# Output projection of a hybrid decoder layer: sums of rows and a factor of the last products on VectorE in place of GpSimd

## The chip, the cores and the metric

The kernel runs on one core of one Trainium2 chip. The metric is the device time of one execution in microseconds (us). The engines in question are TensorE (PE, with PEld for loading its weights), VectorE (DVE), ScalarE (ACT) and GpSimd (POOL). SyncE (SP) issues most of the DMAs. Each engine works through its own list of instructions in order.

## The reference

One layer of a decoder for 2048 prompt tokens and 8 x 4 sample tokens of width 1024. Four groups of heads (convolution, pooling, stick-breaking attention, attention to a memory) each give 512 columns. They are concatenated, multiplied by `w_out`, normalised, added to the input, and normalised once more:

```python
h = rms_norm(x, pre_g); z = h @ w_in
...
mix = jnp.concatenate([y_c * jax.nn.silu(cg), y_p * jax.nn.silu(pg),
                       y_s * jax.nn.silu(sg), y_m * jax.nn.silu(mg)], axis=-1)   # rows x 2048
out = rms_norm(mix @ w_out, post_g)                                               # rows x 1024
x = x + out
...
y = rms_norm(x, final_g)
```

The change lies in `mix @ w_out` and in the factor `post_g` behind it. Nothing ahead of that is touched.

## The kernel before

The output projection is the last stage of the kernel. The 2048 prompt rows are 16 tiles of 128, taken as eight pairs, i = 0 to 7. (i = 8, `LAST`, stands for the 32 sample rows.) A pair of row tiles, the two halves of `mix`'s 2048 columns and the two halves of the 1024 result columns make a 2 x 2 block product, and the kernel computes it with seven block products in place of eight, in a form of Strassen's method: products 1, 7, 2, 6, 4, 5 and 3, whose inputs are blocks or sums of blocks. The sums of the blocks of `w_out` are made earlier. The rows of `mix` lie in DRAM (`mixd`). The row sums are made here, product by product:

- product 7 takes a difference of two blocks, made on POOL (line 1737) and stored to DRAM (`msd[0]`);
- product 6 takes a first difference of that stored one, made on DVE (line 1739, tile `mr6_i_h`);
- a second difference, of product 2's rows and the one of line 1739, is made on POOL (line 1740, tile `mr2_i_h`) and stored to DRAM (`msd[1]`), from where product 3 loads it later;
- product 5 takes the sum of two blocks which product 4's load has brought in one buffer. It is made on POOL (line 1733, tile `mr4_i_h`, the name of the buffer) inside `tc.issue_after(keep["sixth"])`, which keeps it in the order of the source behind the latest difference of line 1740.

In the names, the first number is the product, the second the pair i, the third h, which half of the K dimension (1024 columns, two times 512) it is.

Each input is split into two parts of reduced precision (fp32r), whose products add up to fp32. For the rows ACT rounds (line 1748, tile `mh`) and DVE subtracts (line 1759, tile `ml`); for the weights ACT rounds (line 1654, `wohi`) and DVE subtracts (line 1659, `wolo`). PE then runs three matmuls for each 128 columns of K (line 2024: hi x hi, lo weights x `mh`, hi weights x `ml`), so 12 for one (product, i, h) and 24 for one accumulator `acc`.

The order of the products is a list: product 1 for all i, then 7, then 2 and 6 in turn, then the last three, 4, 5 and 3, in turn pair by pair (from i = 3 on, 4, 5, 3 of a pair follow one another). Rows are loaded three parts ahead, sums made and rounded a few parts ahead. PE's list follows the order of the source. For the other engines a scheduling layer sorts what is recorded, by its estimate of when each instruction can run, unless `tc.keep_in_program_order` or `tc.issue_after` fixes it: the subtractions of line 1739 and the roundings and subtractions of the weights are fixed, while the subtractions of line 1759 are not.

Behind each accumulator DVE adds what the other products gave (lines 1794 to 1811, `U`, `c` and `acc`), ACT takes the sum of squares, and DVE multiplies by `gpost` (line 1816). Of the even row tiles, the first half of the result columns is done early (product 2), stored in DRAM (`c11d`) and loaded back as `oh2_i`; `out_factor` multiplies it by `gpost` on POOL (line 1844). Then `out_tile` finishes a row tile: root of the mean square (from tile 10 on, on POOL, lines 1857 and 1858), `x` + result (line 1868, twice, on DVE), a second root, and the final factor (line 1875, on DVE; `oxt` is the tile that goes out). POOL's other work in this time is these roots and sums of the convolution.

Of the kernel before, what the change touches and what calls it, by code (L numbers as in the profile page):

```python
# [13 lines left out]
ALU = mybir.AluOpType  # L14
# [78 lines left out]
def kernel(  # L93
# [9 lines left out]
    pe, act, dve, pool, sp = nc.tensor, nc.scalar, nc.vector, nc.gpsimd, nc.sync  # L103
# [1544 lines left out]
    def store(key=None):  # L1648
        while len(stores) > 2 or key in [k for k, *_ in stores]:
            sp.dma_start(*stores.pop(0)[1:])  # L1650
# [76 lines left out]
    def out_combine(x):  # L1727
        prod, i, h = x
        store()
        ts = raws[x]  # L1730
        if prod == 5 and i < LAST:
            with tc.issue_after(keep["sixth"]):
                pool.tensor_tensor(out=ts[1], in0=ts[0], in1=ts[1], op=ALU.add)
            ts = ts[1:]
        elif prod == 7:
            pool.tensor_tensor(out=ts[0], in0=ts[0], in1=ts[1], op=ALU.subtract)
            stores.append(((0, i, h), msd[0, i, h], ts[0]))
        elif prod == 6:
            tc.keep_in_program_order(dve.tensor_tensor(out=ts[0], in0=ts[0], in1=ts[1], op=ALU.subtract))
            keep["sixth"] = pool.tensor_tensor(out=ts[2], in0=ts[2], in1=ts[0], op=ALU.subtract).ins  # L1740
            stores.append(((1, i, h), msd[1, i, h], ts[2]))
        raws[x] = ts[0]

# [21 lines left out]
    def out_ready(prod, i, o):  # L1765
# [35 lines left out]
        else:  # L1801
# [28 lines left out]
            if prod == 5 and i != 2 or (prod, i) == (3, 1):  # L1830
                out_factor(2 if prod == 3 else i)
# [9 lines left out]
        keep[2 * i, 0] = c  # L1841

    def out_factor(i):
        pool.tensor_tensor(out=keep[2 * i, 0], in0=keep[2 * i, 0], in1=gpost[:, :512], op=ALU.mult)

    def out_tile(t, a, b):

# [130 lines left out]
    raws, mix, accs, keep, stores = {}, {}, {}, {}, []  # L1978
# [3 lines left out]
    def side_work():  # L1982
        nonlocal opm, conv
        with tc.tile_pool(name="sm", bufs=1, side="left", reuse_waits="tile") as sm2:
            yield from sample_end(sm2, side_ps, S)
        with tc.tile_pool(name="wsp", bufs=1, side="left", reuse_waits="tile") as wsp:
            yield from weight_sums(wsp)
        opm = ox.enter_context(tc.tile_pool(name="opm", bufs=1, side="left", reuse_waits="tile"))
        yield from out_weights(1, opm, pool)
        while (3, 0) not in flags:  # L1990
            yield
        for x in lead_:
            out_load(x)
            out_combine(x)
            out_high(x)
            out_low(x, pool)
            yield

        while (3, 1) not in flags:
            yield  # L2000
        for x in parts[2 * LEAD : 2 * LEAD + 3]:
            out_load(x)
        cp = cx.enter_context(tc.tile_pool(name="cp", bufs=1, side="left", reuse_waits="tile"))
        conv = conv_post(cp, lambda n: conv_ps[0](n), lambda: cx.enter_context(
            tc.tile_pool(name="cpw", bufs=1, side="left", reuse_waits="tile")))
        while "centered" not in flags:
            next(conv)
            yield
# [55 lines left out]
    op = oy.enter_context(tc.tile_pool(name="op", bufs=1, side="right", reuse_waits="tile"))  # L2064
# [58 lines left out]
    def prepare(n):  # L2123
        for d, f in ((3, out_load), (1, out_combine), (0, out_high)):
            for x in parts[: n + d]:
                if x in ready[d]:
                    continue
                prod, i, h = x
                if d == 3 and not h and prod == 2:
                    while i < LAST and ("conv", i) not in flags:  # L2130
                        next(conv, None)
                    if i == LAST:
                        for _ in conv:
                            pass
                f(x)
                ready[d].add(x)

    ready = {d: set(lead_ if d < 3 else parts[: 2 * LEAD + 3]) for d in (3, 1, 0, -1)}
    for n, x in enumerate(parts):
        if n == last_:  # L2140
# [3 lines left out]
            gpost = ope.tile([P, D], F32, name="gpost", bufs=1)  # L2144
# [4 lines left out]
        prod, i, h = x  # L2149
# [55 lines left out]
```

## Time and profile before

| | |
|---|---|
| median of 3 runs | 2327.63 us (2325.99, 2327.63, 2337.69) |
| the profiled execution's own time | 2329.11 us |
| its span | 2327.4 us |
| instructions in it | 43469 |
| HBM read, written | 465.35 MB, 90.72 MB |

The page's groups give for each kind of instruction: line, engine, operation, result <- inputs, how many, then busy time and mean length of one, and after the bar the idle time ahead of them with the engine or DMA that ended most of it. In a timeline a row begins with the start in us and the length; the brackets at its end hold the idle time ahead of the row and what released it. Two instructions merged in one row carry x2. The profile's busy share over 40 slices shows where in the span the stage lies: POOL, busy for most of the span, is at 20 to 40% in the last seven slices, from about 1920 us on:

```
PE   7999999999999999999999999999999999999997
DVE  5343786969647764477786867899999876686997
POOL 3554546556474655545546455489999964432332
```

### The profile page before, as it was taken

The numbers are of one execution on the slowest core, as the hardware profiler recorded it, in microseconds if no ns is written. First come the engines' busy times: TensorE is split into PE (matmuls) and PEld (weight loads), VectorE is DVE, ScalarE is ACT, GpSimd is POOL, SyncE is SP. The second block draws the span as 40 slices with busy tenths as digits, with TensorE's granted clock in tenths as the row PEclk, the third lists the DMA queues.
The fourth block names the chain that finished last, engine by engine and source line by source line (L and its number), as shares of the span: only waits on it lengthen the run. The fifth ranks groups of instructions, "written<-read, shape, count | busy, mean of one in ns | idle before, by whom it ended". The sixth has DMA issues, their size and how long they took to land. (4 is left out here: it accounts for less than half of the span.)

```text
span 2327.4 us, 43469 instructions
## 1 busy us (share of the span) xinstructions
PE 2252.0 (97%) x16512; PEld 1815.3 (78%) x16512; DVE 1716.6 (74%) x2303; ACT 1079.3 (46%) x1975; POOL 1317.9 (57%) x1410
## 2 busy tenths in 40 slices
PE   7999999999999999999999999999999999999997
PEld 7998888888888777777777777667766668787775
DVE  5343786969647764477786867899999876686997
ACT  5332343342442322224242334588888876453553
POOL 3554546556474655545546455489999964432332
PEclk9999999999999999999999999899999999999999
DMA  6689977878679899987977884666545207876774
GB/s 213 200 284 323 337 265 261 285 249 286 245 254 307 308 355 335 336 287 270 319 253 233 298 275 149 166 199 200 158 132 133 76 20 233 290 231 190 248 248 145
DMA packets 338189, 558.32 MB, mean 240 GB/s; under 512 B 29163, under 2 KB 213611, under 8 KB 321581
## 3 DMA queue, kind: packets, MB, share of 16 engines
q1 hardware_dynamic: 282604, 286.83, 39.8%
q0 software_dynamic: 55376, 268.72, 32.4%
q8 instruction: 130, 2.13, 0.4%
q14 instruction: 79, 0.64, 0.1%
HBM read 465.35 MB, written 90.72 MB: 239 GB/s over the span
## 5 line engine op out<-in xcount | busy, mean ns | idle before, releaser
L990 DVE STREAM_TRANSPOSE T<-kt 128x1024 f32<-128x1024 f32 x256 | 308.6, 1226 | 182.2 <-PE sSA L1003 174.7
L957 POOL DMA_INDIRECT vt<-in_cache_v_dram,idv x256 | 253.1, 989 | 257.0 <-PE sO L1042 195.9
L642 DVE SCALAR_TENSOR_TENSOR cacc<-U,par,cacc 128x512 f32<-128x512 f32 x480 | 359.8, 750 | 11.0
L1379 POOL TENSOR_TENSOR be<-be,E 128x512 f32<-128x512 f32 (+4 forms) x316 | 314.1, 1004 | 25.4 <-DVE E L1370 13.0
L957 POOL DMA_INDIRECT kt<-in_cache_k_dram,idk x128 | 128.7, 1006 | 196.1 <-DVE T L990 155.2
L1370 DVE TENSOR_TENSOR_SCAN E<-gam,cr,ZM 128x513 f32<-128x513 f32 x192 | 230.7, 1261 | 4.7 <-POOL csq L1490 1.0
L2024 PE MATMUL acc<-wohi,mh 128*128 128x512 f32 (+1 forms) x480 | 192.0, 400 | 0.2 <-ACT mh L1748 0.2
L2024 PE MATMUL acc<-wolo,mh 128*128 128x512 f32 (+1 forms) x480 | 188.4, 392 | 0.7 <-DVE wolo L1659 0.7
L2024 PE MATMUL acc<-wohi,ml 128*128 128x512 f32 x448 | 177.2, 395 | 6.5 <-DVE ml L1759 6.5
L1400 ACT COPY at<-AT 128x512 f32<-128x512 f32 (+1 forms) x288 | 154.6, 598 | 44.2 <-PE AT L1398 39.0
L1398 PE MATMUL AT<-ident,be 128*128 128x128 f32 x1082 | 155.9, 283 | 17.4 <-ACT at L1400 11.7
L1398 PEld LDWEIGHTS AT<-ident,be 128*128 128x128 f32 x1082 | 122.1, 144 | 59.6 <-issue 23.8
L1298 ACT ACTIVATE be<-S 128x1024 f32<-128x1024 f32 (+1 forms) x158 | 154.2, 976 | 9.9 <-PE S L1293 7.5
L1003 PE MATMUL sSA<-T,W 128*32 128x128 f32 x4096 | 138.2, 276 | 1.8 <-DVE T L990 1.4
L1410 PE MATMUL av<-at,V 128*64 128x256 f32 (+1 forms) x1152 | 137.0, 378 | 0.5 <-DVE sgt L1414 0.3
L1292 PE MATMUL S<-kh,Q 128*128 128x512 f32 (+1 forms) x316 | 134.6, 430 | 1.5 <-ACT be L1298 1.5
L1003 PEld LDWEIGHTS sSA<-T,W 128*32 128x32 f32 x4096 | 104.5, 109 | 36.7 <-issue 29.1
L1759 DVE TENSOR_TENSOR ml<-mr,mh 128x512 fp32r<-128x512 f32 x108 | 92.3, 862 | 40.4 <-ACT mh L1748 39.6
L1410 PEld LDWEIGHTS av<-at,V 128*64 128x64 f32 x1152 | 76.4, 138 | 58.4 <-issue 23.5
L1042 PE MATMUL sO<-vt,saT 128*32 128x512 f32 x1024 | 122.0, 592 | 0.0
L1293 PE MATMUL S<-kl,Q 66*128 66x512 f32 (+1 forms) x316 | 120.7, 386 | 0.0
L1748 ACT CAST mh<-mr 128x512 fp32r<-128x512 f32 (+1 forms) x120 | 70.3, 594 | 89.9 <-PE acc L2024 26.0
(591 smaller groups left out, 6254.5 us busy)
## 6 DMA issues: line engine op xcount, KB each, us to landing
mr<-mixd SPq DMA_DIRECT2D x32, 512.0 KB
Q<-qd SPq DMA_DIRECT2D x96, 128.0 KB
mr<-mixd SPq DMA_DIRECT2D x48, 256.0 KB
xtp<-in_x_prompt_dram SPq DMA_DIRECT2D x16, 512.0 KB
kh<-kd SPq DMA_DIRECT2D x64, 128.0 KB
ws<-in_w_out_dram SPq DMA_DIRECT2D x16, 512.0 KB
wsd<-ws SPq DMA_DIRECT2D x16, 512.0 KB
msd<-mr SPq DMA_DIRECT2D x32, 256.0 KB
```

Of the source, the lines that this page charges most:

```text
L642: dve.scalar_tensor_tensor(out=ps, in0=U[:, a + k : a + k + H], scalar=wd[:, k : k + 1], in1=ps, op0=ALU.mult, op1=ALU.add)
L957: pool.indirect_dma_start(out=dst, out_offset=None, in_=rows, in_offset=bass.IndirectOffsetOnAxis(ap=idx, axis=0))
L990: S["turn"] = dve.transpose(T[:, 2 * hh : 2 * hh + 2].rearrange("p s j t -> p (s j t)"), kt[:, 2 * hh : 2 * hh + 2].rearrange("p s j d -> ...
L1003: pe.matmul(sSs[n][32 * g : 32 * g + 32, P * ml : P * (ml + 1)], lhsT=W[:, jj, :], rhs=T[:, :, jj, :], start=i == 0, stop=i == 3, tile_pos ...
L1292: pe.matmul(S[:, j, :w], lhsT=Q[:, 0, c], rhs=kts[0][:, :w], start=True, stop=False)
L1298: act.activation(out=be, in_=S[:, :, :w], func=AF.Sigmoid)
L1370: dve.tensor_tensor_scan(out=E[:, j][:, ::-1], data0=g_[:, j][:, ::-1], data1=ZM[:, 0:1].to_broadcast([P, 513]), initial=carry[hh, q2][:, ...
L1379: newest.append(pool.tensor_tensor(out=be[:, j, :m], in0=be[:, j, :m], in1=E[:, j, 513 - w : 513 - w + m], op=ALU.mult).ins)
L1398: pe.transpose(ap_[:, n : n + P], A[hp, qb, kc, hh, qt][:, P * r : P * (r + 1)], ident)
L1400: act.copy(at[:, :n], ap_[:, :n])
L1410: pe.matmul(av[64 * hh : 64 * hh + 64, c], lhsT=V[:, 4 * kc + r, 64 * hh : 64 * hh + 64], rhs=ats.pop((hp, qb, kc, hh, q2, r)), start=dg a ...
L2024: pe.matmul(o[:rows], lhsT=m[a][:, k, :rows], rhs=W[prod, 4 * h + k][w], start=not cont and h == k == n == 0, stop=h == 1 and k == 3 and n ...
```

## The change

Three operations of the last products move from POOL to DVE, 40 instructions in all: the sum of product 5 (line 1733, 16 times), the second difference of product 6 (line 1740, 16 times) and the factor of the rows loaded back from DRAM (line 1844, 8 times). The sum of product 5 is also no longer kept behind the latest second difference; the scheduling layer is free to place all three. Nothing else is edited. One line goes, so line numbers behind it are one lower in the new kernel (1732, 1739 and 1843 for the three).

```diff
@@ -1729,15 +1729,14 @@
         store()
         ts = raws[x]
         if prod == 5 and i < LAST:
-            with tc.issue_after(keep["sixth"]):
-                pool.tensor_tensor(out=ts[1], in0=ts[0], in1=ts[1], op=ALU.add)
+            dve.tensor_tensor(out=ts[1], in0=ts[0], in1=ts[1], op=ALU.add)
             ts = ts[1:]
         elif prod == 7:
             pool.tensor_tensor(out=ts[0], in0=ts[0], in1=ts[1], op=ALU.subtract)
             stores.append(((0, i, h), msd[0, i, h], ts[0]))
         elif prod == 6:
             tc.keep_in_program_order(dve.tensor_tensor(out=ts[0], in0=ts[0], in1=ts[1], op=ALU.subtract))
-            keep["sixth"] = pool.tensor_tensor(out=ts[2], in0=ts[2], in1=ts[0], op=ALU.subtract).ins
+            dve.tensor_tensor(out=ts[2], in0=ts[2], in1=ts[0], op=ALU.subtract)
             stores.append(((1, i, h), msd[1, i, h], ts[2]))
         raws[x] = ts[0]
 
@@ -1841,7 +1840,7 @@
         keep[2 * i, 0] = c
 
     def out_factor(i):
-        pool.tensor_tensor(out=keep[2 * i, 0], in0=keep[2 * i, 0], in1=gpost[:, :512], op=ALU.mult)
+        dve.tensor_tensor(out=keep[2 * i, 0], in0=keep[2 * i, 0], in1=gpost[:, :512], op=ALU.mult)
 
     def out_tile(t, a, b):
```

PE's list is the same in both kernels, row by row. POOL's list has 40 rows fewer. DVE's has 40 more, and other rows around them are placed anew. The first difference in DVE's list stands at the first instruction of line 1739, at 2046 us of the profiled execution.

Place one is in DVE's list, ahead of the subtraction `ml6_7_1` for product 6 of the last pair. Before:

```order
L1739 TENSOR_TENSOR mr6_7_1_22850<-mr6_7_1_22850 128x512
L1659 TENSOR_TENSOR wolo4_6_22917<-wor4_6_22832,wohi4_6_22916 128x512
L1659 TENSOR_TENSOR wolo5_1_22922<-wor5_0_22834,wohi5_1_22921 128x512
L1759 TENSOR_TENSOR ml6_7_1_22940<-mr6_7_1_22850,mh6_7_1_22939 128x512
L1659 TENSOR_TENSOR wolo4_7_22946<-wor4_6_22832,wohi4_7_22945 128x512
L1659 TENSOR_TENSOR wolo5_2_22950<-wor5_2_22866,wohi5_2_22949 128x512
```

And in the new kernel (line 1732 is product 5's sum, line 1739 the second difference, line 1758 the subtraction for the rows):

```order
L1738 TENSOR_TENSOR mr6_7_1_22850<-mr6_7_1_22850 128x512
L1732 TENSOR_TENSOR mr4_0_0_22875<-mr4_0_0_22875 128x512
L1739 TENSOR_TENSOR mr2_7_1_22697<-mr2_7_1_22697,mr6_7_1_22850 128x512
L1659 TENSOR_TENSOR wolo4_6_22917<-wor4_6_22832,wohi4_6_22916 128x512
L1659 TENSOR_TENSOR wolo5_1_22922<-wor5_0_22834,wohi5_1_22921 128x512
L1659 TENSOR_TENSOR wolo4_7_22946<-wor4_6_22832,wohi4_7_22945 128x512
L1659 TENSOR_TENSOR wolo5_2_22950<-wor5_2_22866,wohi5_2_22949 128x512
L1758 TENSOR_TENSOR ml6_7_1_22940<-mr6_7_1_22850,mh6_7_1_22939 128x512
```

A row sum for product 4/5 and a second difference stand ahead of the subtraction now, and two subtractions of weights (`wolo4_7`, `wolo5_2`) that followed it precede it.

Place two is in DVE's list as well, from the end of tile 11 (`oxt11`) to the rows of pair 6. `acc3_5` is the accumulator of product 3 of pair 5; lines 1811 and 1816 add `U2` to it and multiply it by `gpost`. Before:

```order
L1868 SCALAR_TENSOR_TENSOR oxt11_23991<-acc4_5_23917,oss_23024,oxt11_23991 128x512
L1868 SCALAR_TENSOR_TENSOR oxt11_23991<-acc5_5_23956,oss_23024,oxt11_23991 128x512
L1759 TENSOR_TENSOR ml5_6_0_24059<-mr4_6_0_23931,mh5_6_0_24058 128x512
L1875 SCALAR_TENSOR_TENSOR oxt11_23991<-oxt11_23991,oss_23024,gfin_23021 128x1024
L1811 TENSOR_TENSOR acc3_5_24007<-acc3_5_24007,U2_20491 128x512
L1759 TENSOR_TENSOR ml5_6_1_24080<-mr4_6_1_23951,mh5_6_1_24079 128x512
L1816 TENSOR_TENSOR acc3_5_24007<-acc3_5_24007,gpost_23020 128x512
L1868 SCALAR_TENSOR_TENSOR oxt10_24043<-oh2_5_23915,oss_23024,oxt10_24043 128x512
L1868 SCALAR_TENSOR_TENSOR oxt10_24043<-acc3_5_24007,oss_23024,oxt10_24043 128x512
L1759 TENSOR_TENSOR ml3_6_0_24100<-mr3_6_0_24021,mh3_6_0_24099 128x512
```

In the new kernel (each line number one lower):

```order
L1867 SCALAR_TENSOR_TENSOR oxt11_23991<-acc4_5_23917,oss_23024,oxt11_23991 128x512
L1867 SCALAR_TENSOR_TENSOR oxt11_23991<-acc5_5_23956,oss_23024,oxt11_23991 128x512
L1810 TENSOR_TENSOR acc3_5_24007<-acc3_5_24007,U2_20491 128x512
L1732 TENSOR_TENSOR mr4_6_1_23951<-mr4_6_1_23951 128x512
L1874 SCALAR_TENSOR_TENSOR oxt11_23991<-oxt11_23991,oss_23024,gfin_23021 128x1024
L1815 TENSOR_TENSOR acc3_5_24007<-acc3_5_24007,gpost_23020 128x512
L1867 SCALAR_TENSOR_TENSOR oxt10_24043<-oh2_5_23915,oss_23024,oxt10_24043 128x512
L1867 SCALAR_TENSOR_TENSOR oxt10_24043<-acc3_5_24007,oss_23024,oxt10_24043 128x512
L1758 TENSOR_TENSOR ml5_6_0_24059<-mr4_6_0_23931,mh5_6_0_24058 128x512
L1758 TENSOR_TENSOR ml5_6_1_24080<-mr4_6_1_23951,mh5_6_1_24079 128x512
L1810 TENSOR_TENSOR acc4_6_24063<-acc4_6_24063,U3_20492 128x512
L1874 SCALAR_TENSOR_TENSOR oxt10_24043<-oxt10_24043,oss_23024,gfin_23021 128x1024
```

The sum for `mr4_6_1` is new on DVE here. The subtractions `ml5_6_0` and `ml5_6_1`, which stood apart among the operations on tiles 11 and 10, stand together behind the two instructions of line 1867 on tile 10, and the last factor of tile 11 (line 1874) comes ahead of both.

## Prediction

> **What bounds the kernel now.** I read the page first, then the busy time by stretches, PE's waits, the groups of VectorE (DVE) and GpSimd (POOL), and the timeline. Line numbers are those of before.
>
> ```profile
> PE 2252.0 (97%) x16512; PEld 1815.3 (78%) x16512; DVE 1716.6 (74%) x2303; ACT 1079.3 (46%) x1975; POOL 1317.9 (57%) x1410
> ```
>
> TensorE (PE) is busy nearly throughout. The order of every engine is unchanged up to DVE's first subtraction at L1739, at 2046 us, so only the last 281 us of the span can move. Columns below: stretch, its length, then busy time and instructions of PE, PEld, DVE, ACT, POOL, the granted clock, DMA share and GB/s.
>
> ```profile
> 2046.00:2100.00 54.00, 51.45 (x277) 43.70 (x276) 46.38 (x74) 28.69 (x59) 23.79 (x22) 1.00 0.73 226
> 2100.00:2161.00 61.00, 60.27 (x295) 49.16 (x295) 42.01 (x62) 22.89 (x47) 13.24 (x10) 1.00 0.72 221
> 2161.00:2200.00 39.00, 37.34 (x162) 29.81 (x160) 36.39 (x57) 22.87 (x48) 18.48 (x9) 1.00 0.72 241
> 2200.00:2250.00 50.00, 48.19 (x206) 36.93 (x207) 47.21 (x84) 27.97 (x78) 14.49 (x9) 1.00 0.71 241
> 2250.00:2314.00 64.00, 60.55 (x257) 47.32 (x255) 55.50 (x83) 28.54 (x76) 17.77 (x25) 1.00 0.54 192
> ```
>
> The clock is full. From 2161 on DVE is as busy as PE: 139.1 of 153 us. What PE itself waits for from 2046 to 2315 (us in total, times, longest):
>
> ```profile
> PE acc L2024 <- DVE ml L1759: 6.5, 10, 1.4
> PE cz L1535 <- DVE cgt L1538: 2.7, 2, 2.0
> PE acc L2024 <- DVE wolo L1659: 0.7, 1, 0.7
> PE acc L2024 <- ACT mh L1748: 0.2, 1, 0.2
> ```
>
> That is 10.1 us, nearly all on DVE. Its work otherwise is fixed, so **10.1 us is the most that this stage can give**. The end is PE's last run of products and the sums behind it:
>
> ```profile
> 2294.62 19.27 PE acc L2024 x82
> 2313.91 0.70 DVE og L1811
> ```
>
> 82 matmuls in 19.27 us are 0.235 each: what PE needs when nothing keeps it.
>
> **What is removed from POOL.** The three groups, with the idle time ahead of them:
>
> ```profile
> L1733 POOL TENSOR_TENSOR mr<-mr 128x512 f32<-128x512 f32 x16 | 27.1, 1707 | 55.0 <-DVE oxt L1868 28.3 <-DMA mr<-mixd 16.6 <-DVE acc L1816 8.8
> L1740 POOL TENSOR_TENSOR mr<-mr,mr 128x512 f32<-128x512 f32 x16 | 27.1, 1693 | 55.0 <-DVE mr L1739 47.7 <-ACT junk L1763 3.9 <-issue 2.7
> L1844 POOL TENSOR_TENSOR oh<-oh,gpost 128x512 f32<-128x512 f32 x8 | 12.4, 1554 | 19.4 <-DMA oh<-c11d 16.1 <-DVE oss L1860 1.7 <-DVE ml L1759 1.7
> ```
>
> Forty instructions, 66.6 us. POOL waits for others before them, and no row of PE's waits names POOL; their removal alone gives nothing there. What it gives is on DVE:
>
> ```profile
> 2167.79 5.24 POOL L1733 TENSOR_TENSOR mr<-mr 128x512 f32<-128x512 f32 x3
> 2168.30 1.77 DVE L1759 TENSOR_TENSOR ml<-mr,mh 128x512 fp32r<-128x512 f32 x1
> 2170.00 0.68 DVE L1794 TENSOR_TENSOR U<-acc,U 128x512 f32<-128x512 f32 x1
> ```
>
> While POOL works, a subtraction with both inputs in SBUF takes 1.77 us, and one that reads an accumulator stays at 0.68. DVE's groups from 2046 to 2314 say the same:
>
> ```profile
> L1759 DVE TENSOR_TENSOR ml<-mr,mh 128x512 fp32r<-128x512 f32 x77 | 65.8, 860 | 7.2 <-ACT mh L1748 6.7
> L1659 DVE TENSOR_TENSOR wolo<-wor,wohi 128x512 fp32r<-128x512 f32 x30 | 27.5, 940 | 1.2 <-ACT wohi L1654 1.1
> L1739 DVE TENSOR_TENSOR mr<-mr 128x512 f32<-128x512 f32 x16 | 13.1, 822 | 0.0
> L1875 DVE SCALAR_TENSOR_TENSOR oxt<-oxt,oss,gfin 128x1024 f32<-128x1024 f32 x14 | 21.1, 1507 | 4.3 <-POOL oss L1858 4.3
> L1739 DVE TENSOR_TENSOR mr<-mr x16: 673/680/1784, 2046.3 to 2160.0; 128x512 f32<-128x512 f32 x16
> ```
>
> The last row gives shortest, median and longest: 0.68 is the undisturbed length, and L1875 takes 1.28 undisturbed (row at 2291.60 below). The excess is 77 x 0.18 + 30 x 0.26 + 16 x 0.14 + 14 x 0.23 = 13.9 + 7.8 + 2.2 + 3.2 = 27.1 us. Of POOL's 87.8 us in this time 66.6 belong to the moved groups (76%), the rest to convolution sums and roots that stay. So the relief is between 20.6 and 27.1 us; I take 24, the middle, since smaller groups that I left out are stretched too.
>
> [...]
>
> **What is added to DVE.** Forty additions, subtractions and products of 128x512. In an undisturbed run of DVE one follows the other every 0.60 us, though each is shown with 0.68:
>
> ```profile
> 2178.34 0.68 DVE L1759 TENSOR_TENSOR ml<-mr,mh 128x512 fp32r<-128x512 f32 x1
> 2178.94 0.67 DVE L1784 TENSOR_TENSOR both<-both,gpost 32x512 f32<-32x512 f32 x1
> 2179.54 0.68 DVE L1811 TENSOR_TENSOR acc<-acc,U 128x512 f32<-128x512 f32 x1
> ```
>
> 40 x 0.60 = 24.0 us, 24 of them (14.4 us) after 2161. Against 24 us of relief **DVE's load stays as it is, within some 4 us**. Time can then only come from where the load lies: before, 1.1 us falls on whichever subtraction is at work; now 0.6 lies where the order puts it. I walked two places.
>
> Place one, the second subtraction for product 6 of pair 7. PE waits there and just behind; the three long DVE rows are the stretches ahead of it:
>
> ```profile
> 2149.13 1.78 DVE L1659 TENSOR_TENSOR wolo<-wor,wohi 128x512 fp32r<-128x512 f32 x1
> 2153.45 1.78 DVE L1739 TENSOR_TENSOR mr<-mr 128x512 f32<-128x512 f32 x1
> 2155.75 2.39 DVE L1659 TENSOR_TENSOR wolo<-wor,wohi 128x512 fp32r<-128x512 f32 x2
> 2162.52 0.50 PE L2024 MATMUL acc<-wohi,ml 128*128 128x512 f32 x1 [0.26 <-DVE ml L1759]
> 2166.12 0.50 PE L2024 MATMUL acc<-wohi,ml 128*128 128x512 f32 x1 [0.54 <-DVE ml L1759]
> ```
>
> The order puts a row addition, a row difference and two weight subtractions more ahead of it, and with the three earlier differences of pairs 6 and 7 five moved and two shifted ones are new: 7 x 0.60 = 4.2 us; three stretches of 1.1 go (3.3). It comes 0.9 later: I count 1.0 for the pair in place of 0.80. **Loss 0.2.**
>
> Place two, pair 6 of products 5 and 3:
>
> ```profile
> 2281.09 1.41 DVE L1868 SCALAR_TENSOR_TENSOR oxt<-acc,oss,oxt 128x512 f32<-128x512 f32 x2 [0.38 <-POOL oss L1858]
> 2283.16 0.50 PE L2024 MATMUL acc<-wohi,ml 128*128 128x512 f32 x1 [0.29 <-DVE ml L1759]
> 2284.48 1.29 DVE L1875 SCALAR_TENSOR_TENSOR oxt<-oxt,oss,gfin 128x1024 f32<-128x1024 f32 x1 [1.38 <-POOL oss L1858]
> 2287.01 0.50 PE L2024 MATMUL acc<-wohi,ml 128*128 128x512 f32 x1 [0.85 <-DVE ml L1759]
> 2290.29 0.50 PE L2024 MATMUL acc<-wohi,ml 128*128 128x512 f32 x1 [0.24 <-DVE ml L1759]
> 2291.60 1.28 DVE L1875 SCALAR_TENSOR_TENSOR oxt<-oxt,oss,gfin 128x1024 f32<-128x1024 f32 x1 [0.75 <-POOL oss L1858]
> 2291.86 2.16 POOL L1844 TENSOR_TENSOR oh<-oh,gpost 128x512 f32<-128x512 f32 x1 [0.29 <-DMA oh<-c11d]
> 2292.80 1.76 DVE L1759 TENSOR_TENSOR ml<-mr,mh 128x512 fp32r<-128x512 f32 x1
> 2294.62 0.50 PE L2024 MATMUL acc<-wohi,ml 128*128 128x512 f32 x1 [1.26 <-DVE ml L1759]
> ```
>
> Four waits, 2.64 us. The last is the moved factor at work: it stretches the subtraction behind it to 1.76. In the new order the subtractions for PE go in pairs behind the tile's work. From the end of product 3 of pair 5 PE needs ml5_6_0 after 24 + 2 matmuls, 6.1 us. DVE does in that time: the accumulator's sum until 0.95 (the pair at L1868 ends about 0.35 in), the row addition until 1.55, then waits for the root until 2.4 (2.72 behind the second L1868, as from 2281.76 to 2284.48), L1875 until 3.65, the factor until 4.25, two L1868 until 5.6, the subtraction until 6.2. PE waits 0.1 to 0.25, and the next three subtractions are early, since their pairs stand together. I count 0.25 in place of 2.64. **Gain 2.4.**
>
> The remaining 4.0 us of waits on ml, wolo and mh I haven't walked; one place lost and one gained, so half: **gain 2.0**. The two waits on the convolution's cgt (2.7) stay. Nothing is added at the end: the moved factors stand ahead of the last pair's tiles.
>
> Other edits at nothing: the stores of the differences and the loads that reuse their buffers pass SP behind a DVE instruction that ends no later than POOL's did; the cover is a whole product's distance to the reading load, and without it each would cost what a load takes to land (a few us). ACT's roundings for product 5 now wait for DVE in place of POOL.
>
> **Sum:** 0.2 lost, 2.4 and 2.0 gained: 4.2 us. The profiled execution took 2329.11 (span 2327.4), so 2324.9; the median of the runs, 2327.63, is 1.5 lower and gives 2323.4. I forecast the middle, **2324.2 us**.
>
> **The rivals.**
> - *Nothing is gained* (16%, 2327.6): the walk at place two hangs on a root in time; half a us later at each of the places eats the gain. For it: the load on DVE is the same. Against: the 1.76 above goes for certain.
> - *All waits on DVE but the convolution's go* (7%): 7.4 us, 2320; with those too, 10.1, 2317.5. For it: DVE's relief may be 27.1. Against: at place one the order puts more ahead.
> - *Tiles run late* (10%, 2331): three pairs have L1875 ahead of a subtraction that PE needs. If the root comes no earlier than before, each costs its wait and itself, 1.38 + 1.28: 8.0 lost against 4.2. It decides if L1875 starts over 2.4 us behind product 3's end.
> - *DVE waits for loads* (7%, 2339.5): POOL sat 16.1 us in five waits for the rows from DRAM and 16.6 in six for mr; DVE is in order, and a wait there holds the subtractions behind it. The rows from DRAM alone would cost 16.1 less the 4.2: 11.9 lost. Against: most moved instructions stand later than POOL ran them. It decides where DVE arrives before the load.
> - *The relief doesn't come* (3%, 2335): then 14.4 us are added after 2161 against 13.9 idle, which lies in waits that only half fill: some 7 lost.
>
> [...]
>
> **How the numbers follow.** 57% for the forecast (2320.5 to 2326.5). The 80% range takes in the full gain of 10.1 and tiles that run late with 2 us of scatter: 2317.5 to 2333. About 0.5% (11.6 us) is what a measurement of this kernel can tell from no change: faster means below 2316, beyond even 10.1; slower means above 2339.3, the late loads at the least. Chances: 2%, 93%, 5%.
>
> **What would show it.** Right: no L1733, L1740 or L1844 on POOL; L1759's mean near 0.69 from 0.86; DVE's busy time after 2161 within 3 us of 139; PE's wait for ml under 4 us from 6.5. Wrong: L1759 still over 0.8; a DMA ahead of the additions on DVE; PE waiting over 1 us at each pair's ml5.

## The result and the profile after

| | before | after |
|---|---|---|
| median | 2333.9 us (17 runs, 2325.99 to 2345.1) | 2324.75 us (17 runs, 2316.09 to 2330.93) |
| ratio, 95% interval | | 0.9958 (0.9945 to 0.9971) |
| the profiled execution's own time, span | 2329.11, 2327.4 us | 2318.57, 2316.9 us |
| first difference of product 6, PE's last product | 2046.30, 2313.87 us | 2043.32, 2302.88 us |
| between the two ("the stage") | 267.57 us | 259.56 us |

The ratio means 9.8 us less, between 6.8 and 12.8. In the two profiles 10.5 us of span are gone. 3.0 of them lie ahead of the first instruction that the change moves, and cannot come from it: in the fourteen profiles of this study that instruction starts anywhere from 2039.4 to 2053.3 us, also where the kernels agree up to there. 8.0 us lie in the stage. What follows PE's last product takes 8.6 us in both, up to DVE's last instruction; the end of the program behind that takes 4.9 us before and 5.4 after, which is why the two differences add up to 0.5 more than the span's. So from here on the stage is the yardstick, and the timed runs stand beside it. It comes from one profiled execution of each kernel, so how far it scatters between executions of the same kernel is not known.

First the page of the changed kernel (in all views of it, line numbers from L1734 on are one lower):

```profile
PE 2245.6 (97%) x16512; PEld 1812.8 (78%) x16512; DVE 1714.0 (74%) x2343; ACT 1079.9 (47%) x1975; POOL 1254.3 (54%) x1370
```

DVE has 40 instructions more and is busy for 2.6 us less. By stretches, the whole stage and its end, columns as in the prediction, before:

```profile
2046.30:2313.87 267.57, 257.50 (x1190) 206.69 (x1188) 227.09 (x354) 130.66 (x305) 87.33 (x72) 1.00 0.68 222
2161.00:2313.87 152.87, 146.08 (x624) 114.06 (x622) 139.01 (x221) 79.38 (x200) 50.61 (x43) 1.00 0.64 221
```

and after:

```profile
2043.32:2302.88 259.56, 254.61 (x1190) 207.36 (x1188) 224.80 (x394) 131.87 (x305) 24.25 (x32) 1.00 0.70 229
2161.00:2302.88 141.88, 140.84 (x611) 112.33 (x609) 129.37 (x236) 76.78 (x193) 10.28 (x18) 1.00 0.67 228
```

Over the stage DVE's work is the same, 227.1 and 224.8 us; POOL's is down by 63.1. DVE's groups in the stage after the change:

```profile
L1758 DVE TENSOR_TENSOR ml<-mr,mh 128x512 fp32r<-128x512 f32 x77 | 53.2, 703 | 5.9 <-ACT mh L1747 5.8
L1659 DVE TENSOR_TENSOR wolo<-wor,wohi 128x512 fp32r<-128x512 f32 x30 | 21.0, 715 | 1.6 <-ACT wohi L1654 1.6
L1739 DVE TENSOR_TENSOR mr<-mr,mr 128x512 f32<-128x512 f32 x16 | 12.6, 792 | 0.1
L1732 DVE TENSOR_TENSOR mr<-mr 128x512 f32<-128x512 f32 x16 | 10.9, 679 | 0.0
L1843 DVE TENSOR_TENSOR oh<-oh,gpost 128x512 f32<-128x512 f32 x8 | 5.5, 682 | 0.0
```

A subtraction for the rows takes 0.703 us on average in place of 0.860, one for the weights 0.715 in place of 0.940. The last three rows are the moved ones; no DMA stands among what they wait for. What PE waits for in the stage:

```profile
PE acc L2023 <- DVE ml L1758: 3.2, 3, 1.2
PE cz L1535 <- DVE cgt L1538: 1.8, 2, 1.5
```

5.0 us in 5 waits, of 10.1 in 14. That explains 5 of the 8 us. The rest is in how a wait is counted. PE's timeline before, around one of them:

```profile
2164.95 0.39 PE L2024 MATMUL acc<-wohi,mh 128*128 128x512 f32 x1
2165.18 0.40 PE L2024 MATMUL acc<-wolo,mh 128*128 128x512 f32 x1
2166.12 0.50 PE L2024 MATMUL acc<-wohi,ml 128*128 128x512 f32 x1 [0.54 <-DVE ml L1759]
2166.45 0.40 PE L2024 MATMUL acc<-wohi,mh 128*128 128x512 f32 x1
```

Matmuls start every 0.23 us. Over this wait the distance is 0.94, and over the next 0.33: 1.27 us for two distances that otherwise take 0.47, so 0.8 lost where the waits' view shows 0.54. The idle time is counted from the modelled end of the matmul before (2165.18 + 0.40), not from 2165.41, when the next was due, and the matmul behind the wait is late too. So I add up, over the stage, what each distance between starts has above 0.233 us (where it is over 0.27), and call it **PE's loss**. It is 15.1 us before and 7.5 after: 7.6 less, nearly all of the 8.0.

By places (us lost, before and after): place one 1.33 and 1.25; place two 3.70 and 1.30; the convolution's cgt 2.95 and 2.06; the other waits on DVE and ACT 5.37 and 1.43; distances without idle time shown 1.79 and 1.50.

### The profile page after: what moved, and what is told of

The parts are those of the page before. It is cut to its first block, busy times and chain, and to the rows that moved or that the text cites. A ratio compares the mean times of both kernels' runs of the same rounds, so it can differ in the third digit from the quotient of the medians.

```text
span 2316.9 us, 43399 instructions
## 1 busy us (share of the span) xinstructions
PE 2245.6 (97%) x16512; PEld 1812.8 (78%) x16512; DVE 1714.0 (74%) x2343; ACT 1079.9 (47%) x1975; POOL 1254.3 (54%) x1370
## 4 chain that ended last, share of the span: by engine, by line
PE 76%; DVE 12%; issue 4%; DMA 3%; ACT 3%; POOL 2%; SPq 0%; another core or an unknown queue 0%; DVEq 0%; ACTq 0%; POOLq 0%
PE acc L2023 11%; PE sSA L1003 5%; PE sO L1042 4%; DVE E L1370 3%; PE AT L1398 3%; PE av L1410 3%; PE z0k L251 2%; PE z1ca L251 2%; PE z1mg L251 2%; PE z1cb L251 2%; PE z1q L251 2%; PE z1v L251 2%; PE z1pu L251 2%; PE z0v L251 2%; PE z0pu L251 2%
## 5 line engine op out<-in xcount | busy, mean ns | idle before, releaser
L1398 PEld LDWEIGHTS AT<-ident,be 128*128 128x128 f32 x1082 | 120.1, 142 | 58.8 <-issue 23.5
L1758 DVE TENSOR_TENSOR ml<-mr,mh 128x512 fp32r<-128x512 f32 x108 | 80.7, 759 | 39.3 <-ACT mh L1747 39.1
```

The source lines that it names most:

```text
L1398: pe.transpose(ap_[:, n : n + P], A[hp, qb, kc, hh, qt][:, P * r : P * (r + 1)], ident)
```

## The experiments

All twelve, each one profile and several timed runs. "Stretch" is what DVE instructions in the stage have above the undisturbed length of their shape, added up where it is over 0.2 us and a POOL instruction overlaps.

| | stage | PE's loss | stretch | ratio to before (95%) |
|---|---|---|---|---|
| before | 267.6 | 15.1 | 30.8 | 1 |
| after | 259.6 | 7.5 | 6.6 | 0.9958 (0.9945 to 0.9971) |
| left_out | 252.4 | 1.0 | 3.0 | 0.9916 (0.9899 to 0.9934) |
| echo | 274.9 | 20.8 | 23.5 | 1.0043 (1.0028 to 1.0058) |
| in_order | 259.9 | 7.9 | 6.6 | 0.9965 (0.9948 to 0.9981) |
| a_only (sum) | 264.9 | 12.6 | 20.4 | 0.9986 (0.9971 to 1.0001) |
| b_only (difference) | 266.4 | 14.3 | 23.4 | 1.0004 (0.9987 to 1.0021) |
| c_only (factor) | 268.2 | 15.3 | 28.0 | 1.0014 (0.9996 to 1.0032) |
| ab (sum and difference) | 258.3 | 6.4 | 10.9 | 0.9961 (0.9942 to 0.9980) |
| dup | 280.4 | 28.1 | 5.4 | 1.0075 (1.0050 to 1.0099) |
| conv_dve | 257.7 | 6.9 | 0.0 | 0.9971 (0.9953 to 0.9990) |
| roots | 257.6 | 5.7 | 6.4 | 0.9954 (0.9937 to 0.9970) |
| conv_last | 257.4 | 5.6 | 3.0 | 0.9965 (0.9946 to 0.9983) |
| acc_dma | 261.5 | 9.5 | 6.1 | 0.9962 (0.9946 to 0.9979) |

Stage less PE's loss is 251 to 253 us in all but echo (254.2), and these 252 are what PE needs. So the question is each time what makes PE's loss. In six runs a part of it is time in which matmuls ran at about half their rate (0.43 us from start to start in place of 0.23 behind a wait of 2.95 us in acc_dma, last section): 4.3 us of the loss in echo, 1.5 in a_only, 1.6 in b_only, 0.8 in c_only, 1.7 in dup and 1.5 in acc_dma. (In echo the convolution's shorter matmuls were slowed too, with 18 matmuls in 4.3 us at a granted clock of 0.60 where the kernel before had 28 in 4.0 at 1.00: some 2 us that the count misses, an estimate from the 254.2 against 252.) Before, after, left_out, in_order, ab and the three runs of "What is left" have none of it in the stage: the granted clock over the stage is 1.00 in these eight, 0.98 in echo and 0.99 in the other five.

**left_out: neither engine does the work.**

```diff
-            with tc.issue_after(keep["sixth"]):
-                pool.tensor_tensor(out=ts[1], in0=ts[0], in1=ts[1], op=ALU.add)
...
-            keep["sixth"] = pool.tensor_tensor(out=ts[2], in0=ts[2], in1=ts[0], op=ALU.subtract).ins
...
-        pool.tensor_tensor(out=keep[2 * i, 0], in0=keep[2 * i, 0], in1=gpost[:, :512], op=ALU.mult)
+        pass
```

> The kernel before without the forty instructions of GpSimd: product 5 takes one block in place of the sum, product 3 takes product 2's rows in place of the second difference, and the even tiles' first half goes without the post factor. VectorE keeps the order of before and gets nothing added. Stage time here means from the first difference for product 6 to PE's last product (267.6 us before, 259.6 after the change). Theory A (GpSimd's instructions hold VectorE up): VectorE's stretched time falls from 30.8 to about 6.6 us, PE's waits on ml, wolo and mh from 7.4 to under 1.5 us, the stage takes 257 to 260 us, ratio to before 0.995 to 0.996. Theory B (the new order on VectorE makes the gain): the order is that of before, so the waits stay above 4 us and the stage takes 264 to 268, ratio 0.999 to 1.

```profile
2039.44:2291.82 252.38, 252.38 (x1189) 207.67 (x1187) 200.71 (x354) 132.43 (x305) 22.25 (x32) 1.00 0.69 230
```

PE is busy from end to end, in the order of before (but for five rows of DVE's list): that order is good enough when nothing disturbs it. Even the convolution's waits are gone. Beyond theory A: the stage is 5 us shorter than it expected, since it had not counted that the 24 us of added work cost anything. From left_out to before, POOL's forty instructions cost 14.2 us of PE's loss; from left_out to after, the same work on DVE costs 6.5. (This kernel also lacks the handing over between DVE, POOL and ACT.)

**echo: the changed kernel with the disturbance put back.** POOL repeats on half the partitions what DVE has just made; one of three places:

```diff
             dve.tensor_tensor(out=ts[1], in0=ts[0], in1=ts[1], op=ALU.add)
+            pool.tensor_tensor(out=keep["s"][64:].rearrange("p (c t) -> p c t", c=4), in0=ts[1][64:], in1=ts[1][64:], op=ALU.add)
```

> The changed kernel, and GpSimd does 40 additions and products of 64x512 beside it, each on the result that VectorE has just made, into a tile that nobody reads. VectorE's order is that of the changed kernel but for two rows. Theory A: VectorE's stretched time comes back, from 6.6 to 25 to 31 us, on top of the 24 us of added work, and the stage takes longer than before the change: 268 to 276 us, ratio to before 1.000 to 1.004. Theory B: the order is what counts, the stage stays at 259 to 262 us and the ratio at 0.996.

```profile
PE acc L2026 <- DVE ml L1760: 10.7, 6, 3.5
PE cz L1535 <- DVE cgt L1538: 2.6, 2, 2.4
```

Theory A. With DVE's order but for two rows that of the changed kernel, 16.9 us more stretch (less than expected) bring 13.2 us of loss, 4.3 of them through the half rate of matmuls behind long waits, and the kernel is slower than before. Order alone gains nothing. (POOL's roots also stand behind the echoes here.)

**in_order: without the freedom of the order.**

```diff
-            dve.tensor_tensor(out=ts[1], in0=ts[0], in1=ts[1], op=ALU.add)
+            with tc.issue_after(keep["sixth"]):
+                dve.tensor_tensor(out=ts[1], in0=ts[0], in1=ts[1], op=ALU.add)
...
-            dve.tensor_tensor(out=ts[2], in0=ts[2], in1=ts[0], op=ALU.subtract)
+            keep["sixth"] = dve.tensor_tensor(out=ts[2], in0=ts[2], in1=ts[0], op=ALU.subtract).ins
```

> The changed kernel with product 5's sum kept behind the latest second difference, as before: the three operations move to VectorE, the freedom of the order does not come with them. Theory A: stretched time about 6.6 us as in the changed kernel, stage 258 to 262 us, ratio 0.995 to 0.997. Theory B: half of the gain or more is lost, stage 263 to 267, ratio 0.998 to 1.

0.35 us of stage: the freedom is worth nothing measurable.

**One part alone, and two.** The edits of a_only, b_only and c_only against the kernel before, in this order; ab has the first two, the difference as in the change:

```diff
-            with tc.issue_after(keep["sixth"]):
-                pool.tensor_tensor(out=ts[1], in0=ts[0], in1=ts[1], op=ALU.add)
+            dve.tensor_tensor(out=ts[1], in0=ts[0], in1=ts[1], op=ALU.add)
```

```diff
-            keep["sixth"] = pool.tensor_tensor(out=ts[2], in0=ts[2], in1=ts[0], op=ALU.subtract).ins
+            keep["sixth"] = dve.tensor_tensor(out=ts[2], in0=ts[2], in1=ts[0], op=ALU.subtract).ins
```

```diff
-        pool.tensor_tensor(out=keep[2 * i, 0], in0=keep[2 * i, 0], in1=gpost[:, :512], op=ALU.mult)
+        dve.tensor_tensor(out=keep[2 * i, 0], in0=keep[2 * i, 0], in1=gpost[:, :512], op=ALU.mult)
```

> Only product 5's sum moves to VectorE, free of the order; the second difference and the factor stay on GpSimd. Theory A: the relief is that of this part, 8.6 of the 24 us of stretch, against 9.6 added; the stage gains at its share, 1 to 4 of the 8 us: 264 to 267, ratio 0.998 to 1. Theory B: this is the part that is set free, so it alone brings most of the gain: 259 to 262, ratio 0.996.

> Only the second difference of product 6 moves to VectorE (product 5's sum stays on GpSimd, behind the latest difference). In the four traces so far the stage is 252 us and what PE loses: 15.1 lost before, 7.5 after the change, 12.6 with the sum alone, 1.0 with nothing of it on either engine. Theory A: the parts add up, this one takes 10.0 of the 24 us of stretch and adds 9.6: PE loses 11 to 13.5 us, stage 263 to 266, ratio 0.998 to 0.999. Theory C (the parts pay only together, since any GpSimd instruction left still hits a subtraction that PE waits for): PE loses 13.5 to 15.5, stage 266 to 268.

> Only the post factor moves to VectorE. Theory A: 6.5 of the 24 us of stretch go for 4.8 us added, the last wait of 1.26 us (behind the factor on GpSimd) goes: PE loses 12 to 14 us, stage 264 to 266.5. Theory C: 14 to 15.5, stage 266 to 268.

> The sum and the second difference on VectorE, the factor left on GpSimd. Singly the sum, the difference and the factor took 2.6, 0.8 and -0.1 us off PE's loss of 15.1, together 7.6. Theory A (parts add up): PE loses 11.5 to 12 us, stage 263.5 to 264.5, ratio 0.998 to 0.999. Theory C (an instruction left on GpSimd runs into the next subtraction instead, so parts pay once most are gone): PE loses 8 to 10.5, stage 260 to 263, ratio 0.996 to 0.998.

As measured the parts do not add up: 2.6, 0.8 and -0.1 us off the loss, 3.4 for sum and difference by addition, 8.8 when both move, more than theory C gave. a_only lies in theory A's range, b_only and c_only lie in theory C's by their loss. But much of what is missing is the half rate of matmuls: without it the three parts would take 4.1, 2.4 and 0.7 us off, 6.5 for the first two and 7.2 for all, where the whole change took 7.6. So these profiles do not show that the relief itself fails to add up, only that a half move can leave one wait long enough to slow what follows. The stretch gives a second, smaller reason: moving the difference alone takes 16 of 40 instructions off POOL, but only 7.4 of 30.8 us of stretch, since the sums left there then hit DVE more often (15 of them in place of 12). DVE and POOL of b_only at place one:

```profile
2165.97 4.66 DVE L1659 TENSOR_TENSOR wolo<-wor,wohi 128x512 fp32r<-128x512 f32 x4
2170.55 0.68 DVE L1759 TENSOR_TENSOR ml<-mr,mh 128x512 fp32r<-128x512 f32 x1
...
2165.78 1.42 POOL L1733 TENSOR_TENSOR mr<-mr 128x512 f32<-128x512 f32 x1 [0.29 <-DMA mr<-mixd]
2168.11 1.36 POOL L1733 TENSOR_TENSOR mr<-mr 128x512 f32<-128x512 f32 x1 [0.91 <-DMA msd<-mr]
```

Four subtractions of weights that take 2.48 us in the changed kernel take 4.66, and PE loses 4.0 us here at once behind the longer queue of moved work: here a half move has both costs in one place, and the half rate behind it costs another 1.6. The factor's move, by contrast, brought nothing: ab loses 1.2 us less than the whole change, though the timed runs don't tell the two apart.

**dup: the added work twice.** The three echoes of above, on DVE in place of POOL:

```diff
-            pool.tensor_tensor(out=keep["s"][64:].rearrange("p (c t) -> p c t", c=4), in0=ts[1][64:], in1=ts[1][64:], op=ALU.add)
+            dve.tensor_tensor(out=keep["s"][64:].rearrange("p (c t) -> p c t", c=4), in0=ts[1][64:], in1=ts[1][64:], op=ALU.add)
```

> The changed kernel with another 40 VectorE instructions of 64x512 that add or multiply each result just made into a tile that nobody reads: the added work doubled, to 48 us. With nothing on either engine PE lost 1.0 us, with 24 us on VectorE 7.5. Theory A (added work costs in proportion, 0.27 us for each us): PE loses 13 to 16 us, stage 265 to 268, ratio near 1.000. Rival (VectorE's idle time in the stage, 35 us, is nearly used up): PE loses 18 to 25 us, stage 270 to 277, ratio 1.002 to 1.005.

```profile
2051.34:2331.71 280.37, 258.52 (x1190) 207.84 (x1188) 254.15 (x434) 133.54 (x305) 24.80 (x32) 0.99 0.65 212
```

The rival is the nearer one, and the loss lies beyond its range too. DVE's busy time in the stage is 200.7 us without the work, 224.8 with it and 254.2 here, so the echoes cost 29 us and not the 24 that were meant. Added work of 0, 24 and 53 us costs 1.0, 7.5 and 28.1 us of loss; DVE is then busy for 80%, 87% and 91% of the stage. It is not an even rise: one wait of 6.11 us, with the half rate behind it (granted clock 0.60 over 4.5 us), makes 8 of the 28.1. (Its order differs in some hundred rows too, so load and order are not told apart here.)

**What is left of the disturbance** (conv_dve, conv_last: the convolution's sums on DVE, all or those of the squares of the last two blocks; roots: those of tiles 10 to 13 on ACT and DVE, as those of the earlier tiles). conv_dve, then conv_last, then roots, each against the changed kernel:

```diff
-                    pool.tensor_tensor(out=sums[i], in0=sums[i] if c else ys[i][:, 0, :N], in1=ys[i][:, c + 1, :N], op=ALU.add)
+                    dve.tensor_tensor(out=sums[i], in0=sums[i] if c else ys[i][:, 0, :N], in1=ys[i][:, c + 1, :N], op=ALU.add)
...
-                pool.tensor_tensor(out=sq[a], in0=sq[a], in1=sq[b], op=ALU.add)
+                dve.tensor_tensor(out=sq[a], in0=sq[a], in1=sq[b], op=ALU.add)
```

```diff
-                pool.tensor_tensor(out=sq[a], in0=sq[a], in1=sq[b], op=ALU.add)
+                (dve if i >= len(blocks) - 2 else pool).tensor_tensor(out=sq[a], in0=sq[a], in1=sq[b], op=ALU.add)
```

```diff
-        fast = 2 * FAST <= t < 16
+        fast = 14 <= t < 16
```

> The changed kernel with the convolution's sums (of four parts and of their squares) on VectorE too; only the roots stay on GpSimd in this stage. Theory A: the 6.6 us of stretch that are left go for some 6 us added (15 sums of 256 or 288 columns in the stage), and the wait of 1.17 us on ml at 2096 goes, whose subtraction stood behind two stretched differences: PE loses 4.5 to 6.5 us, stage 256.5 to 259, ratio to before 0.994 to 0.996. Rival: the sums now wait in VectorE's line and delay the convolution, whose cgt PE waits for: PE loses 8 us or more, ratio 0.996 to 0.999.

> The changed kernel with the sums of squares of the convolution's last two blocks on VectorE. Theory A: the stretch of 6.6 us falls to about 2, the wait of 1.17 us at 2096 falls under 0.5, PE loses 6 to 7 us in place of 7.5, stage 257.5 to 259. Rival: the wait moves to cgt or to the next subtraction and the loss stays at 7 to 8.5.

> The changed kernel with the roots of tiles 10 to 13 taken on ScalarE and VectorE as those of the earlier tiles, in place of GpSimd. In the changed kernel GpSimd's first root step of tile 10 takes 1.39 us in place of 0.30, beside the last factor on VectorE, and PE then waits 1.04 us for ml5_6_0 at 2275. Theory A (VectorE holds GpSimd up as GpSimd holds VectorE up): that wait goes or falls under 0.4 us, PE loses 5.5 to 7 us in place of 7.5, stage 257.5 to 259.5. Rival (the order, not the root, puts the subtraction late): the wait stays near 1 us and PE loses 7 to 9.

All three shorten the stage by about 2 us. conv_last does a part of it where it was expected (1.43 us lost at 2096 in the changed kernel become 0.63, of 1.9 less in all). conv_dve has no stretch left, but a loss of 6.9, just above what theory A allowed: it also moves convolution sums ahead of the stage, and its runs are no faster than the change's. In roots the wait for ml5_6_0 is gone, but the scheduling layer also placed both subtractions ahead of the tile's instructions there, so this run doesn't tell the root from the order. None of the three is faster than the change beyond the intervals. The last two together were not tried.

**acc_dma: product 5's sum by a DMA.**

```diff
+            if prod == 4:
+                pool.dma_start(slot[:, 1].rearrange("p (c t) -> p c t", c=4), mixd[own, 2 * i + 1], accum_op=ALU.add)
...
-            dve.tensor_tensor(out=ts[1], in0=ts[0], in1=ts[1], op=ALU.add)
```

> The changed kernel without product 5's sum on any engine: a DMA that GpSimd issues adds the second block onto the first in the buffer. VectorE keeps 14.4 of the 24 us of added work. With 0, 24 and 48 us added PE lost 1.0, 7.5 and 28.1 us. Theory A (VectorE's load sets the loss): PE loses 3 to 5.5 us, stage 255 to 257.5, ratio to before 0.992 to 0.995. Rival (the summed rows land late, or the issue on GpSimd holds VectorE up): PE waits on mh of product 5, loses 8 us or more, ratio 0.996 or more.

DVE's work falls to 216.7 us, but one wait of 2.95 us, with about 1.5 us more lost behind it (last section), comes in at place one. ACT's waits and DVE's timeline:

```profile
ACT wohi L1654 <- DMA wor<-wsd: 6.9, 2, 5.4
```

```profile
2165.03 0.69 DVE L1759 TENSOR_TENSOR ml<-mr,mh 128x512 fp32r<-128x512 f32 x1
2170.78 0.69 DVE L1659 TENSOR_TENSOR wolo<-wor,wohi 128x512 fp32r<-128x512 f32 x1 [5.06 <-ACT wohi L1654]
2171.38 0.68 DVE L1759 TENSOR_TENSOR ml<-mr,mh 128x512 fp32r<-128x512 f32 x1
```

The subtraction for the rows stands behind one for weights that are not there yet: neither theory had named this. Whether the added DMAs delayed the weights or the changed order of SP's list did stays open.

## Why the prediction was right or wrong

The forecast was 2324.2 us and the median is 2324.75; but the median of before is 2333.9 over 17 runs, not 2327.63 over three. What is to be judged is the gain: 4.2 us forecast within the profiled execution, 8.0 measured in the stage, 6.8 to 12.8 by the ratio. That the forecast time lies within 0.6 us of the median is luck: the time it started from was 6.3 us below the median of before, and the gain was too small by about as much.

- **Relief and addition on DVE, right.** 24 us of relief taken: 30.8 less 6.6 is 24.2. DVE's load "stays as it is, within some 4 us": 2.3. So the gain comes from where the load lies, as the prediction put it, and left_out and echo show it from both sides.
- **"10.1 us is the most that this stage can give": the step that failed.** PE's loss was 15.1, since a wait costs it more than the idle time shown (at place one 1.33 us for two waits that show 0.80, some 0.27 more for each), and distances without idle time shown cost 1.79. left_out took 14.2 us of it away and its stage is 15.2 us shorter. Of the loss of 5.1 beyond what the view shows, the change took 2.5.
- **Place one, right.** 1.0 us of idle time forecast, 0.98 measured. PE's loss there went from 1.33 to 1.25 us, as one wait took the place of two.
- **Place two, right in kind, short by 0.8.** 0.25 us forecast, 1.04 measured. The walk had L1874 (its L1875) start 2.4 us behind the end of product 3, the root for the pair behind it in time. DVE, POOL and PE of the changed kernel there:

```profile
2267.57 1.41 DVE L1867 SCALAR_TENSOR_TENSOR oxt<-acc,oss,oxt 128x512 f32<-128x512 f32 x2 [0.38 <-DMA out_dram<-oxt]
2268.89 0.69 DVE L1810 TENSOR_TENSOR acc<-acc,U 128x512 f32<-128x512 f32 x1
...
2271.01 1.28 DVE L1874 SCALAR_TENSOR_TENSOR oxt<-oxt,oss,gfin 128x1024 f32<-128x1024 f32 x1 [0.84 <-POOL oss L1857]
2273.14 0.75 DVE L1867 SCALAR_TENSOR_TENSOR oxt<-oh,oss,oxt 128x512 f32<-128x512 f32 x1 [0.23 <-POOL oss L1857]
2274.47 1.28 DVE L1758 TENSOR_TENSOR ml<-mr,mh 128x512 fp32r<-128x512 f32 x2
...
2271.07 1.39 POOL L1856 TENSOR_SCALAR oss<-ssk 128x1 f32<-128x1 f32 x1
2272.54 0.56 POOL L1857 TENSOR_TENSOR oss<-oss,two 128x1 f32<-128x1 f32 x1
...
2268.08 0.39 PE L2023 MATMUL acc<-wohi,mh 128*128 128x512 f32 x1
...
2275.20 0.50 PE L2023 MATMUL acc<-wohi,ml 128*128 128x512 f32 x1 [1.04 <-DVE ml L1758]
```

  PE's row at 2268.08 is the first behind product 3. The larger part of the 0.8 is there before any root is late: the first pair at L1867 ends 0.8 us behind it, where the walk had 0.35, so L1874 starts 2.9 us behind it and not 2.4, although it follows its pair at the distance that the walk took (2.78 us from the second L1867). The rest is the next root. POOL's first step for it, 0.3 us in the kernel before, starts 0.06 us after DVE's long instruction, takes 1.39 and ends 0.17 us behind it: here DVE holds POOL. The second pair at L1867 waits 0.23 us for that root, and both subtractions wait behind it. So the rival of the late tiles, by its own sign (over 2.4 us), came true at one place of three, and cost about 1 us of its 8.
- **The remaining waits, too small a gain.** Of 4.0 us half was taken to go; 1.2 are left. Of the convolution's 2.7, taken to stay, 1.8 are left.
- **Signs.** L1759's mean near 0.69: 0.703. PE's wait for ml under 4 us: 3.2. DVE's busy time after 2161 within 3 us of 139: wrong, 129.4. The same products begin 4.1 us earlier in the changed kernel, at 2156.9, and from there on DVE is busy for 133.5. The added work fell as I had it (23 rows there, 24 forecast), so the relief fell more on the second half: 139.0 and 13.8 added less 133.5 are some 19 us, of 26 in the stage.
- **Rivals.** Nearest in size was that all waits on DVE but the convolution's go (7.4 us of idle time), though not in kind: three of them stayed. The loads on DVE's path cost nothing, as no DMA stands ahead of the moved instructions.

Why one us of stretch costs PE twice a us of planned work (14.2 us for 27.8 of stretch, 6.5 for 24 of work, from left_out) was not shown by a run of its own. It would follow from the order being made without knowledge of stretch, so that planned work is laid into gaps and stretch is not; that is argued only.

## What to carry to other kernels

Before giving VectorE's spare work to GpSimd, add up what the VectorE instructions beside it have above their undisturbed length: here 66.6 us on GpSimd cost VectorE 24 us, just what the work takes there itself, and the bound engine paid twice for the former. Move enough of such work at once: 16 of the 40 instructions paid 0.8 or 2.6 us, 32 and 40 of them 8.8 and 7.6, though some 1.5 us of each of the first two went to the half rate of matmuls behind one long wait. And stop while VectorE has room: the next 29 us cost 20.6.

## What the runs showed of the hardware that had not been expected

**Behind some long waits the matmuls ran at half their rate.** PE in acc_dma, behind the wait of 2.95 us, and the granted clock there (0.57, the number behind POOL's):

```profile
2172.12 0.50 PE L2024 MATMUL acc<-wohi,ml 128*128 128x512 f32 x1 [2.95 <-DVE ml L1759]
...
2172.77 0.63 PE L2024 MATMUL acc<-wolo,mh 128*128 128x512 f32 x1
2173.19 0.63 PE L2024 MATMUL acc<-wohi,ml 128*128 128x512 f32 x1
2173.62 0.63 PE L2024 MATMUL acc<-wohi,mh 128*128 128x512 f32 x1
```

```profile
2172.00:2176.00 4.00, 3.88 (x10) 3.05 (x11) 4.00 (x8) 2.21 (x4) 0.83 (x1) 0.57 1.05 390
```

Matmuls start every 0.43 us in place of 0.23 for some 3.5 us, which costs about 1.5 us on top of the wait. The same follows the waits of 2.34 and 3.53 us in echo, 2.60 in a_only and 3.62 in b_only (clock 0.60 to 0.67 over the 4 to 5 us behind); behind one of 2.00 in echo it was 0.59, but behind waits of 2.12 and 2.34 in dup 1.00. So the length alone does not decide; what does is not shown.

**VectorE held GpSimd too.** A root step of 0.3 us in the kernel before took 1.39 beside a VectorE instruction of 1.28 in the changed kernel (the rows at place two; the same step took 1.39 in conv_last too).
